# Gated DeltaNet layer: the 16x16 blocks of two visits solved in one set of vector operations

## The chip, the cores and the metric

The kernel runs on one core of a Trainium2 chip. The metric is the device time of one execution in microseconds (us). Five engines work side by side, each through its own queue in program order: PE (TensorE, matrix products; its weight loads are listed as PEld), DVE (VectorE), ACT (ScalarE), POOL (GpSimd) and SP (SyncE, which issues most transfers).

## What is computed

One layer over 2048 latent tokens and 256 context tokens of width 1024: a modulated LayerNorm, one wide projection, a branch A (gated DeltaNet with 8 heads of 128 in both directions), a branch B (gated short convolution), two output projections that are gated, merged and projected again, and a LayerNorm with the residual. The change lies in branch A:

```python
m = jnp.where(tri_strict, jnp.einsum('bhncd,bhnsd->bhncs', k_beta, k) * decay, 0.0)
eye = jnp.eye(CHUNK, dtype=jnp.float32)
t_inv = lax.linalg.triangular_solve(eye + m, jnp.broadcast_to(eye, m.shape), left_side=True, lower=True)
u = jnp.einsum('bhncs,bhnsv->bhncv', t_inv, v_beta)
w = jnp.einsum('bhncs,bhnsd->bhncd', t_inv, k_beta * jnp.exp(g_cum)[..., None])
...
def step(s, xs):
    qk_i, q_dec_i, k_dec_i, u_i, w_i, d_i = xs
    v_new = u_i - jnp.einsum('bhck,bhkv->bhcv', w_i, s)
    o = jnp.einsum('bhck,bhkv->bhcv', q_dec_i, s) + jnp.einsum('bhcs,bhsv->bhcv', qk_i, v_new)
    s = s * d_i[..., None, None] + jnp.einsum('bhck,bhcv->bhkv', k_dec_i, v_new)
    return s, o
```

The scan runs forward and backward over the same tokens. For each chunk and head a unit triangular matrix is inverted (lower in one direction, upper in the other).

## The kernel before, in words

Three stages follow each other. Up to about 1820 us the kernel computes the projections and writes their results to DRAM. Then comes the loop of branch A. After it `final` computes the last products.

The loop works on chunks of 128 tokens. A visit is one chunk in one direction, for all 8 heads; 18 chunks in two directions make 36 visits, forward (d = 0) and backward (d = 1) in turn. Each direction keeps its state `S`. A chunk that has been seen in the other direction takes its products of keys and queries from DRAM (`again`).

A visit needs, in this order: its keys and cumulative decays loaded (`visit_load`), the decay matrix `gcb` (`visit_decay`: eight operations of DVE at L140 between two exponentials of ACT, and a product `qd` on POOL at L138), the triangular matrix `N` (`gram`, products on PE, then L167 or L152 on DVE), the inverse of its 16x16 diagonal blocks (`inv_base`), the growth of the inverse from 16 to 32 (`inv_w16`, `inv_d16`), to 64 (`inv_w32`, `inv_d32`) and to 128 (`inv_w64`, `inv_d64`), the products of queries and keys (`gram` of `QK`), and then the steps with the state: `st_ks` (L299, its PSUM tiles emptied by DVE into `vh`, L301), `st_v` (L308), `st_o` (L319, L320) and `st_u` (L327, its PSUM tiles added to `S` by DVE, L332).

`inv_base` runs on DVE. The tile `n16` holds each block's negated strict triangle, 16 columns for 8 heads on 128 partitions. In 15 rounds a row of the growing inverse `R` is copied to all 16 rows of its block (L191, `stream_shuffle`), multiplied by a column of `n16` (L192) and added to `R` (L193). A round with w columns works on 8w elements of each partition, w from 1 to 15. Each of the three operations needs the one before it. At the end ACT spreads `R` to `r32` and DVE transposes it to `r32t` (L198).

The loop over i puts parts of several visits into one step: the state's part of visit i, the growth of the inverse of visit i + 1, `QK` of visit i + 2, and loads, decays, `N` and `inv_base` of visit i + 3. Between them `dense(n)` puts products of the output projections (L1230, L1232, L1234); `FILL` says how many of them a step takes, 24 in most, and a step before a repeated chunk takes 8 more. They run out where the next job's chunks are not yet normalised. All that is left runs after the loop.

PE's order is what the program writes (`manual_schedule`). The other engines' order is made by a planner at compile time, which takes the ready instruction that the program wrote first. PSUM tiles are in short supply: two each for `gram`, the inverse (`pinv`) and the state's products (`pst`), so PE waits where an earlier tile is not emptied yet.

## Time and profile before

| | us |
|---|---|
| median of 3 runs | 3288.05 |
| lowest and highest | 3284.26, 3294.42 |
| the profiled execution, its time | 3284.18 |
| its span, first to last instruction | 3282.5 |

The profile is of one execution. Times in its rows count from the start of the span. Busy time of an engine is the time in which at least one of its instructions ran; PE's matmuls overlap, so a mean duration is longer than the distance between two starts. PEclk is the clock that TensorE was granted, as a share of full speed.

### The profile page before, as it was taken

The page shows a single profiled execution, that of the slowest core. Times are in us where ns is not written, and L with a number is a line of the kernel's source. Part 1 is how long each engine was busy: PE and PEld are TensorE (multiplying, and loading weights), DVE is VectorE, ACT ScalarE, POOL GpSimd, SP SyncE. Part 2 cuts the span into 40 slices and gives each one's busy share as a digit, 9 for nine tenths or more (in the row PEclk, how much of TensorE's full clock was granted, in tenths as well). Part 3 has the DMA queues.
Part 4 walks back from the last instruction along what each step waited for, and adds up shares of the span by engine and source line. Part 5 has one row for each costly group of instructions (what it writes and reads, how often), then busy time and mean ns, then how long its engine had stood idle before and what let it go on. Part 6 is the DMA issues. An engine that isn't in the chain of part 4 may idle for free.

```text
span 3282.5 us, 60541 instructions
## 1 busy us (share of the span) xinstructions
PE 3011.9 (92%) x22089; PEld 2486.6 (76%) x22089; DVE 2294.7 (70%) x5815; ACT 1560.3 (48%) x3453; POOL 1622.7 (49%) x1156
## 2 busy tenths in 40 slices
PE   7899999999998899999999888988888888898987
PEld 4678778888886777888888677877777777786766
DVE  7656645555656564555632678999999898978699
ACT  4564633333456555333434355555555665654221
POOL 3444557765676454666665333344343233425464
PEclk9999999999999999999999889889989888999999
DMA  5433323224564432222333645465566667767742
GB/s 208 136 106 91 101 68 91 81 69 151 180 188 136 113 95 78 65 65 71 97 111 90 228 160 166 162 197 174 168 209 213 209 221 230 223 209 247 225 140 98
DMA packets 423047, 481.75 MB, mean 147 GB/s; under 512 B 25428, under 2 KB 324949, under 8 KB 421724
## 3 DMA queue, kind: packets, MB, share of 16 engines
q1 hardware_dynamic: 413646, 470.43, 45.8%
q10 hardware_dynamic: 9102, 7.45, 0.7%
q8 instruction: 173, 2.83, 0.4%
q14 instruction: 126, 1.03, 0.1%
HBM read 341.32 MB, written 136.47 MB: 146 GB/s over the span
## 4 chain that ended last, share of the span: by engine, by line
PE 50%; DVE 26%; issue 6%; ACT 5%; DMA 4%; POOL 4%; SPq 0%; DVEq 0%; ACTq 0%; POOLq 0%
PE pd L746 12%; PE pd L747 12%; PE pd L748 12%; DVE rb L192 3%; DVE gcb L140 3%; DVE R L193 2%; POOL al L352 2%; DVE rb L191 2%; DMA gcb<-gcd 2%; PE pf L1234 1%; PE pf L1230 1%; PE pf L1232 1%; DVE N L167 1%; PE pst L319 1%; ACT n L177 1%
## 5 line engine op out<-in xcount | busy, mean ns | idle before, releaser
L746 PE MATMUL pd<-bh,ah 128*128 128x512 f32 x2240 | 889.1, 397 | 9.9 <-ACT u L766 5.8
L748 PE MATMUL pd<-bh,al 128*128 128x512 f32 x2240 | 877.7, 392 | 0.0
L747 PE MATMUL pd<-bl,ah 128*128 128x512 f32 x2240 | 876.8, 391 | 0.0
L352 POOL TENSOR_TENSOR al<-s,ah 128x512 fp32r<-128x512 f32 x348 | 478.0, 1376 | 415.1 <-ACT ah L351 402.2
L352 POOL TENSOR_TENSOR al<-raw,ah 128x512 fp32r<-128x512 f32 x260 | 367.6, 1417 | 339.6 <-ACT ah L351 312.8
L746 PEld LDWEIGHTS pd<-bh,ah 128*128 128x128 f32 x2240 | 423.6, 189 | 98.1 <-issue 6.6
L748 PEld LDWEIGHTS pd<-bh,al 128*128 128x128 f32 x2240 | 423.2, 189 | 90.3 <-POOL al L352 0.4
L747 PEld LDWEIGHTS pd<-bl,ah 128*128 128x128 f32 x2240 | 423.6, 189 | 85.5
L351 ACT CAST ah<-s 128x512 fp32r<-128x512 f32 x352 | 215.4, 619 | 335.7 <-PE pd L747 311.2
L351 ACT CAST ah<-raw 128x512 fp32r<-128x512 f32 x264 | 162.4, 617 | 244.9 <-PE pd L747 206.5
L732 DVE TENSOR_TENSOR s<-s,raw 128x512 f32<-128x512 f32 x80 | 111.8, 1397 | 217.8 <-POOL s L732 217.8
L1234 PE MATMUL pf<-ah,wl 128*128 128x512 f32 x512 | 220.6, 431 | 5.6 <-DVE wl L352 3.5
L1230 PE MATMUL pf<-ah,wh 128*128 128x512 f32 x512 | 214.4, 419 | 10.5 <-DVE R L193 4.2
L1232 PE MATMUL pf<-al,wh 128*128 128x512 f32 x512 | 214.5, 419 | 6.1 <-DVE al L352 3.2
L352 POOL TENSOR_TENSOR wl<-wraw,wh 128x1024 fp32r<-128x1024 f32 x48 | 117.0, 2437 | 202.3 <-ACT wh L351 60.8
L192 DVE TENSOR_TENSOR rb<-rb,n 128x8 f32<-128x8 f32 (+6 forms) x540 | 199.9, 371 | 5.0
L140 DVE SCALAR_TENSOR_TENSOR gcb<-gcb,gc,mask 128x128 f32<-128x128 f32 x288 | 180.4, 631 | 6.8 <-ACT qd L137 5.6
L138 POOL TENSOR_TENSOR qd<-qd,qT 128x1024 f32<-128x1024 f32 x32 | 76.2, 2380 | 199.2 <-ACT qd L137 194.3
L193 DVE TENSOR_TENSOR R<-R,rb 128x8 f32<-128x8 f32 (+6 forms) x540 | 159.4, 296 | 5.6
L319 PE MATMUL pst<-S,qd 128*128 128x128 f32 x512 | 113.4, 307 | 36.5 <-ACT ot L1268 18.2
L1008 ACT ACTIVATE t<-t 128x512 f32<-128x512 f32 (+1 forms) x112 | 67.3, 601 | 138.1 <-DVE t L993 138.0
L771 DVE TENSOR_TENSOR u<-pd,u 128x512 f32<-128x512 f32 x80 | 55.0, 687 | 106.5 <-PE pd L748 97.5
(346 smaller groups left out, 6245.3 us busy)
## 6 DMA issues: line engine op xcount, KB each, us to landing
raw<-in_w_in SPq DMA_DIRECT2D x160, 512.0 KB, 3.9
kT<-kTd SPq DMA_DIRECT2D x36, 512.0 KB, 4.5
gcb<-gcd SPq DMA_DIRECT2D x36, 512.0 KB, 4.2
kt<-kd SPq DMA_DIRECT2D x36, 512.0 KB, 4.0
vh<-vd SPq DMA_DIRECT2D x36, 512.0 KB, 3.7
wraw<-in_w_b SPq DMA_DIRECT2D x32, 512.0 KB, 4.7
qT<-qTd SPq DMA_DIRECT2D x32, 512.0 KB, 3.9
wraw<-in_w_a SPq DMA_DIRECT2D x32, 512.0 KB, 4.5
```

Of the source, the lines that this page charges most:

```text
L140: nc.vector.scalar_tensor_tensor(out=gcb[:, h, :], in0=gcb[:, h, :], scalar=gcT[:, h:h + 1], in1=self.mask[d], op0=ALU.subtract, op1=ALU.min)
L192: nc.vector.tensor_tensor(out=rbv, in0=rbv, in1=bc(n16[:, :, i:i + 1], w), op=ALU.mult)
L193: nc.vector.tensor_tensor(out=R[:, :, c0:c1], in0=R[:, :, c0:c1], in1=rbv, op=ALU.add)
L319: nc.tensor.matmul(po[:, j, :], v["qd"][:, h, :], S[:, h, :], start=True, stop=False)
L351: self.nc.scalar.copy(out=hi, in_=src)
L352: (eng or self.nc.gpsimd).tensor_tensor(out=lo, in0=src, in1=hi.bitcast(F32), op=ALU.subtract)
L746: mm(ps, hi[:, k, :], bh, start=(first and k == 0), stop=False, skip_group_check=not first)
L747: mm(ps, hi[:, k, :], bl, start=False, stop=False, skip_group_check=not first)
L748: mm(ps, lo[:, k, :], bh, start=False, stop=(last and k == 3), skip_group_check=not first)
L1230: mm(ps, wh[:, k, :], ah, start=(k == 0), stop=False)
L1232: mm(ps, wh[:, k, :], al, start=False, stop=False)
L1234: mm(ps, wl[:, k, :], ah, start=False, stop=(k == KT - 1))
```

## The change

Two visits, one of each direction, are handed to `inv_base` together. The block of the backward visit is transposed first, so that both are lower triangular, and `n16` and `R` hold both, 16 columns for 16 heads. The rounds go by columns: row j of `n16` is copied to all rows of the block by the shuffle, multiplied by column j of `R` and added to the columns behind j. The shuffle of the next round is written between the multiply and the add of this one, and reads `n16`, not `R`. At the end the transposition that each visit had anyway is taken the other way round for the backward one.

For this `N` of a visit is made one step earlier (visit i + 4 in step i), as are loads, decays and `QK` (i + 3), and the tiles concerned get one more buffer. The loop begins at -4, with 24 dense products in that step. `inv_base` is called in every other step, for visits i + 3 and i + 4.

`inv_w16` reads `N` itself instead of the negated copy `n32`, and its result is negated. In `inv_w32` and `inv_d32` the products of different blocks follow each other head by head, where one block's eight heads came before the next block's; the transposed product is among them. The host call gives a smaller scratch for dynamic DMA.

```diff
-FILL = lambda i: {-3: 24, -2: 84, -1: 56}[i] if i < 0 else 24 if i < 16 else 24 if i < 25 else 27
+FILL = lambda i: {-4: 24, -3: 24, -2: 84, -1: 56}[i] if i < 0 else 24 if i < 16 else 24 if i < 25 else 27
...
-        v["kT"] = self.gk.tile([P, H, P], F32, name="kT", bufs=3)
+        v["kT"] = self.gk.tile([P, H, P], F32, name="kT", bufs=4)
...
-        v[name] = N = self.g2.tile([P, H, P], F32, name=name, bufs=2 if name == "N" else 3)
+        v[name] = N = self.g2.tile([P, H, P], F32, name=name, bufs=3 if name == "N" else 4)
...
-    def inv_base(self, v):
...
-        for i in (range(15, 0, -1) if d == 0 else range(0, 15)):
-            c0, c1 = (i, 16) if d == 0 else (0, i + 1)
-            w = c1 - c0
-            rbv = rb.rearrange("p h c -> p (h c)")[:, 0:H * w].rearrange("p (h c) -> p h c", c=w)
-            nc.vector.stream_shuffle(rbv, R[:, :, c0:c1], [i] * 16 + [16 + i] * 16)
-            nc.vector.tensor_tensor(out=rbv, in0=rbv, in1=bc(n16[:, :, i:i + 1], w), op=ALU.mult)
-            nc.vector.tensor_tensor(out=R[:, :, c0:c1], in0=R[:, :, c0:c1], in1=rbv, op=ALU.add)
...
+    def inv_base(self, va, vb):
+
+        nc, g2 = self.nc, self.g2
+        n16 = g2.tile([P, 2, H, 16], F32, name="n16", bufs=1)
+        for v in (va, vb):
+            n = g2.tile([P, H, 32], F32, name="n32", bufs=1)
+            for g in range(4):
+                s = slice(32 * g, 32 * g + 32)
+                nc.scalar.mul(out=n[s], in_=v["N"][s, :, s], mul=-1.0)
+            if v["d"]:
+                t = g2.tile([P, H, 32], F32, name="n32t", bufs=1)
+                nc.vector.transpose(self.fl(t), self.fl(n))
+                n = t
+            o = n16[:, v["d"]]
+            nc.scalar.mul(out=o, in_=n[:, :, 0:16], mul=self.m16[0])
+            nc.vector.scalar_tensor_tensor(out=o, in0=n[:, :, 16:32], scalar=self.m16[1], in1=o, op0=ALU.mult, op1=ALU.add)
+        n16 = n16.rearrange("p d h c -> p (d h) c")
+        rows = lambda t: t.unsqueeze(1).to_broadcast([P, 2 * H, 16])
+        nc.vector.tensor_tensor(out=n16, in0=n16, in1=rows(self.tri16), op=ALU.mult)
+
+        R = g2.tile([P, 2 * H, 16], F32, name="R16", bufs=1)
+        nc.gpsimd.tensor_copy(out=R, in_=rows(self.i16))
+
+        def row(j):
+            w = 15 - j
+            t = g2.tile([P, 2 * H * 15], F32, name="rb")[:, 0:2 * H * w].rearrange("p (h c) -> p h c", c=w)
+            nc.vector.stream_shuffle(t, n16[:, :, j + 1:16], [j] * 16 + [16 + j] * 16)
+            return t
+
+        nxt = row(0)
+        for j in range(15):
+            t, c = nxt, slice(j + 1, 16)
+            nc.vector.tensor_tensor(out=t, in0=t, in1=bc(R[:, :, j:j + 1], 15 - j), op=ALU.mult)
+            if j < 14:
+                nxt = row(j + 1)
+            nc.vector.tensor_tensor(out=R[:, :, c], in0=R[:, :, c], in1=t, op=ALU.add)
+        for v in (va, vb):
+            v["r32"] = r32 = g2.tile([P, H, 32], F32, name="r32", bufs=3)
+            v["r32t"] = r32t = g2.tile([P, H, 32], F32, name="r32t", bufs=3)
+            r, t = (r32t, r32) if v["d"] else (r32, r32t)
+            for hf in range(2):
+                nc.scalar.mul(out=r[:, :, 16 * hf:16 * hf + 16], in_=R[:, H * v["d"]:H * v["d"] + H], mul=self.m16[hf])
+            nc.vector.transpose(self.fl(t), self.fl(r))
...
-                nc.tensor.matmul(wp[s, h, :], v["n32"][s, h, :], v["r32t"][s, h, :], start=True, stop=True)
+                nc.tensor.matmul(wp[s, h, :], v["N"][s, h, s], v["r32t"][s, h, :], start=True, stop=True)
...
-        for p1, p2 in self.blocks(v["d"], 32):
-            for h in range(H):
+
+        for h in range(H):
+            for p1, p2 in self.blocks(v["d"], 32):
                 nc.tensor.matmul(wp[p2, h, :], v["N"][p1, h, p2], v["r32t"][p1, h, :], start=True, stop=True)
...
+        dt = self.pi.tile([P, H, 32], F32, name="pinv")
+        a, b = blks[lo], blks[1 - lo]
+        for h in range(H):
+            nc.tensor.matmul(dp[a[0], h, :], w32[a[1], h, :], r32[a[1], h, :], start=True, stop=True)
+            nc.tensor.matmul(dp[b[0], h, :], w32[b[1], h, :], r32[b[1], h, :], start=True, stop=True)
+            nc.tensor.matmul(dt[a[1], h, :], r32[a[1], h, :], w32[a[1], h, :], start=True, stop=True)
...
-            for i in range(-3, nv):
+            for i in range(-4, nv):
...
-                if v3:
-                    self.gram(v3, "N", v3["kT"])
-                    self.inv_base(v3)
-                if i > -3:
+                if v4:
+                    self.gram(v4, "N", v4["kT"])
+                    if v4["d"]:
+                        self.inv_base(v3, v4)
+                if i > -4:
                     dense(part[3])
```

## Rows read from the trace of the kernel before

**Rows 1.** The page's first part: busy us of each engine, share, instructions.

```profile
PE 3011.9 (92%) x22089; PEld 2486.6 (76%) x22089; DVE 2294.7 (70%) x5815; ACT 1560.3 (48%) x3453; POOL 1622.7 (49%) x1156
```

**Rows 2.** Stretches: us, busy PE, PEld, DVE, ACT, POOL (instructions), PEclk, DMA share, GB/s.

```profile
1820.00:1897.00 77.00, 61.88 (x552) 48.92 (x552) 57.60 (x224) 32.72 (x62) 28.30 (x17) 0.87 0.73 244
1897.00:2952.00 1055.00, 917.87 (x12562) 811.80 (x12548) 938.52 (x3642) 613.63 (x1451) 386.67 (x254) 0.92 0.60 195
```

**Rows 3.** Chain that ended last, 1900 to 2950 us: shares by line.

```profile
by line: DVE rb L192 9.4%; DVE gcb L140 8.5%; DVE R L193 7.1%; DVE rb L191 4.8%; DMA gcb<-gcd 4.0%; issue 3.5%; ACT n L177 3.3%; PE pst L319 3.3%; DVE N L167 2.9%; PE pst L320 2.6%; DVE QK L167 2.6%; PE pf L1234 2.4%; PE pst L327 2.1%; PE p
```

**Rows 4.** DVE's groups, 2000 to 2900 us: busy us, mean ns | idle before.

```profile
L192 DVE TENSOR_TENSOR rb<-rb,n 128x88 f32<-128x88 f32 (+14 forms) x440 | 159.1, 362 | 3.7
L140 DVE SCALAR_TENSOR_TENSOR gcb<-gcb,gc,mask 128x128 f32<-128x128 f32 x232 | 153.8, 664 | 5.6 <-ACT qd L137 5.6
L193 DVE TENSOR_TENSOR R<-R,rb 128x80 f32<-128x80 f32 (+14 forms) x441 | 125.7, 285 | 4.3
L191 DVE STREAM_SHUFFLE rb<-R 128x16 f32<-128x16 f32 (+14 forms) x440 | 97.3, 222 | 0.0
```

**Rows 5.** Stretch of 2000 to 2900 us, columns as in rows 2.

```profile
2000.00:2900.00 900.00, 781.08 (x10617) 690.95 (x10616) 815.42 (x3169) 522.35 (x1234) 333.65 (x220) 0.92 0.61 200
```

**Rows 6.** Timeline of DVE in one step: start us, us, instruction.

```profile
2297.14 0.34 DVE L167 SCALAR_TENSOR_TENSOR QK<-gram,cc,gcb 128x128 f32<-128x128 f32 x1
2297.40 0.17 DVE L192 TENSOR_TENSOR rb<-rb,n 128x16 f32<-128x16 f32 x1
2297.48 0.34 DVE L167 SCALAR_TENSOR_TENSOR QK<-gram,cc,gcb 128x128 f32<-128x128 f32 x1
...
2300.35 0.45 DVE L226 STREAM_TRANSPOSE r32t<-r 128x256 f32<-128x256 f32 x1
```

**Rows 7.** Timeline of DVE and POOL, 2306 to 2312 us.

```profile
2306.62 2.41 DVE L140 SCALAR_TENSOR_TENSOR gcb<-gcb,gc,mask 128x128 f32<-128x128 f32 x1
2308.96 2.43 DVE L192 TENSOR_TENSOR rb<-rb,n 128x96 f32<-128x96 f32 x1
...
2306.52 2.36 POOL L138 TENSOR_TENSOR qd<-qd,qT 128x1024 f32<-128x1024 f32 x1 [9.53 <-ACT qd L137]
2308.84 2.43 POOL L352 TENSOR_TENSOR wl<-wraw,wh 128x1024 fp32r<-128x1024 f32 x1
```

**Rows 8.** DVE's groups by shape, 1800 to 2960 us (15 shuffle shapes).

```profile
L198 DVE STREAM_TRANSPOSE r32t<-r 128x256 f32<-128x256 f32 x36 | 15.8, 440 | 13.7 <-ACT r L196 13.7
L182 DVE TENSOR_TENSOR n<-n,tri 128x128 f32<-128x128 f32 x36 | 14.0, 389 | 0.1
L191 DVE STREAM_SHUFFLE rb<-R 128x120 f32<-128x120 f32 x36 | 10.1, 281 | 0.0
L191 DVE STREAM_SHUFFLE rb<-R 128x8 f32<-128x8 f32 x36 | 5.8, 162 | 0.0
```

**Rows 9.** Groups of PE, 2000 to 2900 us, columns as in rows 4.

```profile
L319 PE MATMUL pst<-S,qd 128*128 128x128 f32 x464 | 103.8, 309 | 36.5 <-ACT ot L1268 18.2 <-DVE ot L1271 13.9 <-ACT v L311 4.3
L299 PE MATMUL pst<-S,kT 128*128 128x128 f32 x473 | 68.9, 295 | 30.1 <-DVE S L332 19.2 <-DVE ot L1271 10.8
L222 PE MATMUL pinv<-r,w 32*32 32x32 f32 x1856 | 23.1, 200 | 15.9 <-ACT w L213 15.9
```

**Rows 10.** Timeline of PE in one step, 2294 to 2311 us.

```profile
2294.44 0.75 PE L222 MATMUL pinv<-r,w 32*32 32x32 f32 x64 [1.19 <-ACT w L213]
...
2300.85 1.09 PE L246 MATMUL pinv<-r32t,N 32*32 32x32 f32 x32 [0.29 <-DVE r32t L226]
...
2305.50 1.00 PE L259 MATMUL pinv<-r,w32i 32*32 32x32 f32 x29
...
2306.43 0.57 PE L265 MATMUL pinv<-w32i,r 32*32 32x32 f32 x13
...
2310.58 0.39 PE L1234 MATMUL pf<-ah,wl 128*128 128x512 f32 x1
2310.81 0.39 PE L1230 MATMUL pf<-ah,wh 128*128 128x512 f32 x1
```

More of the change, by code (lines that the diff above doesn't have):

```diff
@@ L69, in consts @@
         nc.vector.reduce_sum(idx, pr, axis=AXX)
-        self.tri16 = []
-        for d, op in ((0, ALU.is_gt), (1, ALU.is_lt)):
-            t = pool.tile([P, 16], F32, name=f"tri{d}")
-            nc.vector.tensor_scalar(out=t, in0=io, scalar1=idx, scalar2=None, op0=op)
-            self.tri16.append(t)
+        self.tri16 = pool.tile([P, 16], F32, name="tri")
+        nc.vector.tensor_scalar(out=self.tri16, in0=io, scalar1=idx, scalar2=None, op0=ALU.is_gt)
         self.mask = []
@@ L256, in inv_d32 @@
         blks = self.blocks(d, 32)
-        for p1, p2 in blks:
-            for h in range(H):
-                nc.tensor.matmul(dp[p1, h, :], w32[p2, h, :], r32[p2, h, :], start=True, stop=True)
+        dt = self.pi.tile([P, H, 32], F32, name="pinv")
[4 more added lines that the diff above has]
+            nc.tensor.matmul(dt[a[1], h, :], r32[a[1], h, :], w32[a[1], h, :], start=True, stop=True)
         for p1, _ in blks:
             nc.scalar.mul(out=v["r64"][p1, :, c2], in_=dp[p1], mul=-1.0)
-        p1, p2 = blks[lo]
-        dt = self.pi.tile([P, H, 32], F32, name="pinv")
-        for h in range(H):
-            nc.tensor.matmul(dt[p2, h, :], r32[p2, h, :], w32[p2, h, :], start=True, stop=True)
+        p1, p2 = a
         nc.scalar.mul(out=v["r64t"][p2, :, c1], in_=dt[p2], mul=-1.0)
@@ L1305, in window @@
                     self.inv_w16(v1)
-                if v2 and v2["latent"]:
-                    self.gram(v2, "QK", v2["qT"])
-                if v2 and v2["again"]:
+                if v3 and v3["latent"]:
+                    self.gram(v3, "QK", v3["qT"])
+                if v3 and v3["again"]:
                     dense(8)
-                if v3:
-                    self.visit_load_q(v3)
+                if v4:
+                    self.visit_load_q(v4)
                 if v1:
                     self.inv_d16(v1)
-                if v3:
-                    self.visit_decay(v3)
+                if v4:
+                    self.visit_decay(v4)
                 if v0:
```

35 lines of the change are left out of this document (9 added, 26 removed).

## The prediction

> **What bounds the kernel now.** I read four views. The page first: PE is the busiest engine of the whole run [rows 1], which would say that a change on DVE buys nothing. A share of the whole run averages over stages, so the second view is the busy time by stretch [rows 2]. The stretch from the first product of `st_v` to the last visit's, 1897 to 2952 us, is the one that the change touches; it holds 35 steps from visit to visit of 1055 / 35 = 30.1 us each. In its middle, 2000 to 2900 us, DVE is busy 815.4 of 900 us and PE 781.1 [rows 5]: 27.3 and 26.2 us of a step. Neither is full, so the third view is the chain that ended last within the stretch [rows 3]: its four largest lines are DVE's, the three lines of the 16x16 solve (L191, L192, L193) and the decay line L140, 29.8% together. The fourth is what PE's groups wait for [rows 9]: the first products of a visit (L299) stood 30.1 us for DVE to empty PSUM tiles, those of `st_o` (L319) 36.5 us, 22.5 for ACT and 13.9 for DVE; L222 stood 15.9 us for ACT alone. So DVE sets the pace by its order of work, and PE is a close second, 1.1 us a step below it. That bound on the gain is the main thing to see here.
>
> **The solve on DVE.** Today each visit takes 15 rounds of shuffle, multiply, add, on 8w elements (8 heads, w = 1 to 15 columns). The shuffles show what such an operation costs undisturbed [rows 8]: 162 ns at 8 elements, 281 at 120, so (281 - 162) / 112 = 1.06 ns an element and 154 ns that do not depend on size. Fifteen take 15 x 154 + 1.06 x 960 = 3.33 us. Multiplies and adds cost the same where nothing holds them (0.17 us for 16 elements, [rows 6]). A visit: 3 x 3.33 = 10.0 us, two visits 20.0. Changed, two visits share 15 rounds on 16w elements: 3 x (15 x 154 + 1.06 x 1920) = 13.0 us. The elements are the same; 45 fixed costs are gone. That is 6.9 us a pair, 3.5 a visit, if each fixed cost is paid in full. It isn't always: where independent instructions alternate, the next starts 0.08 us before the last ends [rows 6], and then an operation removed gives back 0.154 - 0.08, 3.3 us a pair or 1.7 a visit. Between 1.7 and 3.5 I take 2.8, nearer to the upper end, because the new order carries its own independent neighbour (the next shuffle reads `n16`, not `R`, and stands between multiply and add), so more of the remaining operations overlap than today.
>
> **Preparation.** The second direction gains a transposition of 128x256, 0.44 us [rows 8]; the two multiplications by the triangle (0.39 us each) become one of twice the size, 0.39 + 128 x 1.06 ns = 0.53, so 0.25 less. Together +0.2 us a pair, 0.1 a visit. The ScalarE multiplications keep their number, with sign and mask moved; ACT is busy 522 of 900 us [rows 5] and hides them. The wait that is added: the first visit of a pair now waits for the second one's `N`. It was made a visit ahead for this, and its products are wanted only two visits later. Behind the waiting instruction on DVE stand `vh`, `QK` and `S`, which fill the time today too.
>
> **Stalls beside POOL.** A `gcb` operation that takes 0.34 us took 2.41, and the multiply after it 2.43 instead of about 0.26, exactly while POOL worked on `qd` and then `wl` [rows 7]. The means tell how often [rows 4]: L140 664 ns against 340, L192 362 and L193 285 against 222 for the shuffles of the same sizes. (324 x 232 + 140 x 440 + 63 x 441) ns = 165 us in 900, 5.5 us a step, half of POOL's 11.2 [rows 5]; 3.0 of it falls on the solve. If stalls go with the number of solve operations, half of that goes, 1.5; if each POOL instruction still meets one victim, nothing does. I take 0.7. The Trainium skill, "SBUF — State Buffer", section "SBUF: two separate sides", says that a VectorE operation with two SBUF inputs and a GpSimd operation that reads SBUF take a lock for the whole instruction and the later one is blocked. These rows agree on the length of a stall (2.4 us for 2.4). By that rule the stall belongs to the POOL instruction and not to the count of VectorE's, so it would put 0 for my 0.7, and the time would be 0.7 x 35 = 24 us higher; that is part of the second rival below.
>
> Sum for DVE: 27.3 - 2.8 + 0.1 - 0.7 = 23.9 us a step on average. It is not even: the pair's solve falls into every other step. Rounds (11 to 13 us), their stalls (some 2) and preparation (some 2) are 15 us, so the steps alternate between 23.9 + 7.5 = 31.4 and 16.4 us of DVE work.
>
> **Products in turn.** Today the 32-to-64 products run tile after tile: 32 matmuls in 1.09 us (L246), 48 in 1.50 from the first of L259 to the last of L265 [rows 10], 34 and 31 ns each. L222 takes four tiles in turn and needs 0.75 us for 64, 12 ns each. In turn over two tiles (L246) or over three products of which two share rows (L259, L265), the 80 matmuls cost between 80 x 12 ns = 0.95 us and today's 2.59. I take half of today's price, 17 ns: 1.36, a gain of 1.2 us a step. PE: 26.2 - 1.2 = 25.0. The Trainium skill, "TensorE: Matmul & The Clock Gate", section "Wait — 56ns, not 53.3ns?", has a floor of about 25 ns from start to start. That would leave only 0.6 us of the gain, but L222's 12 ns are below it, so the row decides.
>
> **Steps.** A light step is PE's: 25.0 plus the waits for ACT that stay, (15.9 + 18.2 + 4.3) / 29.9 steps = 1.3 [rows 9], 26.3 us. A heavy step has 31.4 us of DVE work, but its first part (both preparations, the vh of the next visit) can start in the light step's tail, where DVE has slack; what can't start early is what waits for the second `N`. I give 3 us to that, hence 28.4. Mean 27.4, 2.7 less than today: 35 x 2.7 = 95 us.
>
> **The ends.** The extra round ahead puts 24 more dense matmuls before the first visit, at 0.23 us from start to start [rows 10] 5.5 us. Against it the first two solves, which today keep DVE busy 57.6 of 77 us before the first visit [rows 2], become one; net +2, between -5 and +6. `gram` of QK is a visit further ahead too, its loads and stores with it: the SP queue issues the same transfers in the same order, only for another visit, and one more buffer each covers them. The 8 extra dense matmuls of repeated chunks start a visit earlier, the b jobs run out a visit earlier as well, and then dense work stops until chunks 6 to 9 are normalised. By the counts of `FILL`, the loop holds 1121 dense matmuls instead of 1129; 8 more fall into the end, +2 us. The end itself is untouched.
>
> Sum against the profiled execution (span 3282.5, its time 3284.2 us): 3284.2 - 95 + 2 + 2 = **3193 us**. The median of the three runs, 3288.05, is 3.9 us above that execution, so the forecast is 2.9% below the median, and 0.3%, 10 us, is about what a measurement of this kernel can tell from no change.
>
> **Rivals.**
> PE all through: if the heavy step's surplus fits into the light one's slack, every step is PE's, 25.5 to 26.3 us. For it: DVE's mean, 23.9, is below PE's 25.0, and the stretch's mean granted clock is 0.92 [rows 2], so a part of it ran at the lower level, 1.2 GHz. Against it: DVE runs in order, and the solve starts only behind the second `N`. 35 x 4.2 = 147 us less: 3141.
> Half of it: overlap hides more of the fixed cost than I think (1.7 instead of 2.8) and the stalls stay (0). Heavy steps are then 1.8 x 2 = 3.6 us longer, so the mean falls by 0.9 only: 3284 - 32 + 4 = 3256.
> Nothing of it: stretches of one visit's solve were spread over each step and filled waits; with the long operations DVE wins 3 us a pair, and PE loses as much waiting in heavy steps. For it: DVE and PE are only 1.1 us apart today. 3284, within 10 us.
> Slower: in a heavy step the solve has first call on DVE, as it was emitted first. Today an operation of another kind fits between any two solve operations, so eight `QK` and the two of `inv_d16` pass from 2297.1 to 2300.8, and L246, which needs them, waits 0.3 us [rows 6, 10]. In the new rounds the shuffle takes one of the three places, so only one stranger may pass per round of some 1.2 us; ten strangers take 12 us instead of 4. PE's few matmuls in between cover 2 us of that. L246 then stands about 6 us in every second step, and DVE runs dry later in the same step: 31.4 + 5 and 27 us, a mean of 31.5. 35 x 1.4 = +49: 3333. It decides where L246 waits more than some 5 us in a heavy step. Against it: the long first rounds only begin when `N` is through ACT, and much `QK` work can pass before.
>
> **How the numbers follow.** Forecast (3160 to 3230) 0.55, PE all through 0.17, half 0.13, nothing 0.06, slower 0.09. Faster by over 0.3% is the first three, 0.85; within 0.3% 0.06; slower 0.09. Leaving out the slower case, the empty one and the last of the PE case's gain, the range is 3125 to 3272. The likeliest case's own range is 3160 to 3230.
>
> **What would show it.** The solve's lines at about 13 us of DVE per pair, without stalls, under half as many instructions; shuffles of 240 elements near 0.41 us. DVE's share of the middle of the stretch below PE's. Steps alternating near 28 and 26 us. L246, L259 and L265 together under 1.6 us. L299's wait for DVE gone in light steps. It would be wrong if steps don't alternate, if L246's wait grows instead of L299's falling, or if PE waits for ACT take over what DVE gave back.

## The result, and the profile after

The changed kernel takes 3323.18 us (median, 3315.83 to 3327.75), the kernel before 3286.16 us beside it: ratio 1.0117, with a 95% interval of [1.0093, 1.0141]. It is 1.2% slower; the forecast of 3193 us and its range of 3125 to 3272 us are both missed.

The profiled execution after took 3315.83 us, with a span of 3314.1; it is the fastest of the four, so it shows 31.6 us of loss where the medians show 37. Its page, first part (busy us of each engine):

```profile
PE 2981.9 (90%) x22089; PEld 2447.3 (74%) x22089; DVE 2125.5 (64%) x4735; ACT 1565.9 (47%) x3453; POOL 1629.9 (49%) x1137
```

Both busy engines did less than in [rows 1], DVE by 169 us and PE by 30, and yet the span grew by 31.6 us. So the work did shrink, and waits took more than its place. The same stretches as in [rows 2, 5]: ahead of the first visit, the loop from visit to visit, and its middle.

```profile
1831.00:1916.00 85.00, 65.31 (x621) 51.73 (x620) 58.48 (x178) 39.43 (x75) 37.83 (x22) 0.88 0.75 248
1916.00:2978.00 1062.00, 875.18 (x12463) 770.88 (x12462) 780.47 (x2610) 610.96 (x1436) 374.55 (x232) 0.89 0.59 191
2000.00:2900.00 900.00, 734.80 (x10340) 646.82 (x10338) 664.55 (x2190) 509.71 (x1187) 319.96 (x196) 0.89 0.60 194
```

In the loop DVE is busy 780 us instead of 939 and PE 875 instead of 918, and the loop takes 7 us more. A part of PE's fall is work that left the loop: it holds 906 dense products instead of 938, because 24 went ahead of the first visit and 8 behind the last; at 0.23 us each that is some 7 us. Where the 31.6 us are: 9.6 in the projections ahead of the window (their last product starts at 1830.1 instead of 1820.5 us), 9.0 before the first visit, 6.8 in the loop, 6.3 after the last visit. The steps alternate, as forecast: in the loop 34.4 us for each step with a solve and 26.0 for each without, against 30.2 and 30.0 before. One such pair of steps (stretches as above):

```profile
2216.60:2254.10 37.50, 28.27 (x382) 25.63 (x376) 28.30 (x115) 18.35 (x37) 11.96 (x9) 0.86 0.44 146
2254.10:2280.40 26.30, 24.09 (x384) 21.77 (x376) 18.29 (x46) 14.67 (x31) 9.96 (x7) 1.00 0.61 196
```

In the light step PE works 24.1 of 26.3 us. In the heavy one neither engine is full: PE 28.3 and DVE 28.3 of 37.5 us. So it is first of all a matter of order, not of load. The groups of PE in the middle of the loop, with what they waited for (columns as in [rows 9]):

```profile
L332 PE MATMUL pst<-S,qd 128*128 128x128 f32 x448 | 98.9, 306 | 5.7 <-DVE ot L1284 3.0 <-ACT v L324 1.5 <-ACT ot L1281 1.2
L340 PE MATMUL pst<-v,kt 128*128 128x128 f32 x462 | 65.9, 289 | 21.1 <-DVE S L345 21.1
L312 PE MATMUL pst<-S,kT 128*128 128x128 f32 x456 | 60.6, 289 | 2.2 <-DVE ot L1284 2.2
L300 PE MATMUL pinv<-r,w 64*64 64x64 f32 x464 | 37.6, 239 | 26.7 <-ACT w L293 26.7
L259 PE MATMUL pinv<-r32t,N 32*32 32x32 f32 x928 | 22.7, 203 | 34.5 <-DVE r32t L238 34.5
L1412 PE MATMUL gram<-ident,ot 128*128 128x128 f32 x88 | 19.2, 362 | 26.7 <-ACT ot L1400 26.7
```

L332 and L312 are L319 and L299 of [rows 9]: their waits of 36.5 and 30.1 us fell to 5.7 and 2.2, which is what the forecast hoped for. In their place L259 (L246 of before), L300 and L340 wait, and L1412, which transposes normalised chunks. L259 and most of L300 stand in the first half of the loop, L340 and L1412 in the second. L259's wait is the one of [rows 10], 0.3 us then. Now PE in a heavy step:

```profile
2221.12 0.39 PE L332 MATMUL pst<-S,qd 128*128 128x128 f32 x2
2221.34 0.39 PE L333 MATMUL pst<-v,QK 128*128 128x128 f32 x2
2221.57 1.06 PE L340 MATMUL pst<-v,kt 128*128 128x128 f32 x8
2227.89 1.07 PE L259 MATMUL pinv<-r32t,N 32*32 32x32 f32 x32 [5.26 <-DVE r32t L238]
...
2229.47 0.64 PE L333 MATMUL pst<-v,QK 128*128 128x128 f32 x2
2229.90 0.63 PE L332 MATMUL pst<-S,qd 128*128 128x128 f32 x2
...
2242.24 1.14 PE L300 MATMUL pinv<-r,w 64*64 64x64 f32 x16 [3.63 <-ACT w L293]
```

and DVE in the same time:

```profile
2220.00 0.34 DVE L164 SCALAR_TENSOR_TENSOR QK<-gram,cc,gcb 128x128 f32<-128x128 f32 x1
2220.26 0.36 DVE L200 TENSOR_TENSOR rb<-rb,R 128x208 f32<-128x208 f32 x1
...
2220.55 0.37 DVE L194 STREAM_SHUFFLE rb<-n 128x192 f32<-128x192 f32 x1
2220.82 0.36 DVE L203 TENSOR_TENSOR R<-R,rb 128x208 f32<-128x208 f32 x1
2221.10 0.34 DVE L164 SCALAR_TENSOR_TENSOR QK<-gram,cc,gcb 128x128 f32<-128x128 f32 x1
...
2226.63 0.36 DVE L236 SCALAR_TENSOR_TENSOR r<-pinv,m16h,r 128x128 f32<-128x128 f32 x1
...
2227.38 0.45 DVE L238 STREAM_TRANSPOSE r32t<-r 128x256 f32<-128x256 f32 x1
```

Three operations of a round, then one stranger: eight `QK` go first, one per round of 0.8 to 1.1 us, then the two of `inv_d16` that L259 waits for. This is the mechanism of the "slower" rival. The stand costs a second time: the pairs of products behind it start 0.43 us apart (2229.47, 2229.90), where those ahead of it started 0.22 us apart (2221.12, 2221.34), so 0.21 and 0.11 us for each product. The granted clock of the heavy step is 0.86, of the light one 1.00; from 2226.3, within the stand, to 2233.1 us it is 0.50, which is 1.2 GHz. L259 stands 4.0 to 8.2 us in each of the eight heavy steps in which `QK` is made, 42.8 us together, and 0.3 us at most in any other step of the loop; the later visits load `QK` instead of making it, so no eight strangers queue ahead.

Late work runs on: `qd`'s exponential follows the late `st_o` on ACT, the decay's eight `gcb` follow it on DVE, their exponential on ACT ends at 2241.6, and only behind it in ACT's queue comes the copy that L300 waits for (3.63 us). This wait is not the order's alone: the eight `gcb` take 5.93 us here, because two of them take 1.96 and 2.48 us beside POOL's `wl` (2.37 us) and `qd` (2.46 us). Had these two taken 0.34 us like the other six, all would have been done an estimated 3.8 us earlier, which is as long as the wait; no run separates the two causes.

### The profile page after: what moved, and what is told of

The parts are those of the page before. It is cut to its first block, busy times and chain, and to the rows that moved or that the text cites. A ratio compares the mean times of both kernels' runs of the same rounds, so it can differ in the third digit from the quotient of the medians.

```text
span 3314.1 us, 59462 instructions
## 1 busy us (share of the span) xinstructions
PE 2981.9 (90%) x22089; PEld 2447.3 (74%) x22089; DVE 2125.5 (64%) x4735; ACT 1565.9 (47%) x3453; POOL 1629.9 (49%) x1137
## 4 chain that ended last, share of the span: by engine, by line
PE 52%; DVE 19%; issue 9%; DMA 6%; POOL 6%; ACT 4%; SPq 0%; DVEq 0%; POOLq 0%; ACTq 0%
PE pd L759 12%; PE pd L761 12%; PE pd L760 12%; POOL al L365 3%; DVE gcb L137 2%; DMA gcb<-gcd 2%; DVE R L203 2%; DVE rb L194 1%; DVE rb L200 1%; PE gram L155 1%; PE pf L1247 1%; POOL s L745 1%; DVE t L1004 1%; PE pf L1243 1%; PE pst L332 1%
## 5 line engine op out<-in xcount | busy, mean ns | idle before, releaser
L365 POOL TENSOR_TENSOR al<-raw,ah 128x512 fp32r<-128x512 f32 x260 | 376.5, 1450 | 329.0 <-ACT ah L364 289.3
L745 DVE TENSOR_TENSOR s<-s,raw 128x512 f32<-128x512 f32 x80 | 97.1, 1214 | 218.6 <-POOL s L745 199.5
L137 DVE SCALAR_TENSOR_TENSOR gcb<-gcb,gc,mask 128x128 f32<-128x128 f32 x288 | 188.0, 706 | 26.3 <-ACT qd L134 24.9
L1243 PEld LDWEIGHTS pf<-ah,wh 128*128 128x128 f32 x512 | 103.6, 202 | 41.3 <-issue 12.5
L1247 PEld LDWEIGHTS pf<-ah,wl 128*128 128x128 f32 x512 | 103.3, 202 | 34.5 <-DVE wl L365 10.8
L1245 PEld LDWEIGHTS pf<-al,wh 128*128 128x128 f32 x512 | 103.0, 201 | 32.2 <-DVE al L365 5.9
```

Of the source, the lines that this page charges most:

```text
L137: nc.vector.scalar_tensor_tensor(out=gcb[:, h, :], in0=gcb[:, h, :], scalar=gcT[:, h:h + 1], in1=self.mask[d], op0=ALU.subtract, op1=ALU.min)
L365: (eng or self.nc.gpsimd).tensor_tensor(out=lo, in0=src, in1=hi.bitcast(F32), op=ALU.subtract)
L745: eng.tensor_tensor(out=o, in0=a, in1=b, op=op)
L1243: mm(ps, wh[:, k, :], ah, start=(k == 0), stop=False)
L1245: mm(ps, wh[:, k, :], al, start=False, stop=False)
L1247: mm(ps, wl[:, k, :], ah, start=False, stop=(k == KT - 1))
```

## The experiments

Each is the changed kernel, or the kernel before, with the edit shown. The planner orders each engine's queue by priority: operations under `high_priority(600)` come earlier in it, under a negative number later. All ratios are against the kernel before, run beside it. Stages of the profiled execution, in us: start of the last product of the projections, from there to the first visit (its first product of `st_v`), mean step of the first 18 and of the last 17, and the end behind the last visit's `st_v`.

| kernel | ratio [95%] | proj. | to first visit | steps 1-18 | steps 19-35 | end |
|---|---|---|---|---|---|---|
| before | 1 | 1821 | 77 | 30.9 | 29.3 | 330 |
| after | 1.0117 [1.0093, 1.0141] | 1830 | 86 | 31.1 | 29.5 | 336 |
| e1_turn_only | 0.9944 [0.9922, 0.9965] | 1815 | 78 | 30.2 | 29.1 | 329 |
| e2_ahead_alone | 0.9997 [0.9981, 1.0012] | 1818 | 92 | 30.3 | 28.7 | 337 |
| e3_d16_first | 0.9995 [0.9981, 1.0010] | 1827 | 89 | 28.1 | 30.6 | 336 |
| e4_solve_last | 1.0206 [1.0180, 1.0233] | 1825 | 89 | 31.8 | 30.5 | 337 |
| e5_pad | 1.0096 [1.0075, 1.0117] | 1816 | 86 | 31.2 | 29.6 | 339 |
| e6_pad_fill0 | 1.0083 [1.0065, 1.0100] | 1817 | 89 | 31.3 | 29.4 | 336 |
| e7_state_first | 1.0018 [1.0007, 1.0029] | 1817 | 88 | 29.9 | 29.7 | 336 |
| e8_gate_first | 1.0051 [1.0033, 1.0069] | 1814 | 88 | 30.7 | 29.8 | 338 |
| e12_d16_pad | 0.9951 [0.9934, 0.9968] | 1816 | 89 | 28.3 | 30.7 | 337 |
| e9_both_first | 0.9855 [0.9832, 0.9877] | 1817 | 83 | 27.0 | 29.4 | 339 |
| e13_turn_order | 0.9925 [0.9907, 0.9943] | 1820 | 78 | 29.7 | 29.2 | 330 |
| e15_ahead_order | 0.9936 [0.9913, 0.9958] | 1820 | 90 | 29.3 | 28.9 | 336 |
| e10_half_each | 0.9898 [0.9876, 0.9920] | 1817 | 84 | 27.7 | 29.6 | 337 |
| e11_half_later | 0.9823 [0.9805, 0.9842] | 1820 | 88 | 27.4 | 29.0 | 339 |
| e14_half_gone | 0.9766 [0.9734, 0.9798] | 1817 | 82 | 27.5 | 27.6 | 339 |
| e16_norm_first | 0.9844 [0.9824, 0.9864] | 1819 | 86 | 26.9 | 29.0 | 337 |

**The parts of the change.** e1 is the kernel before with the products in turn:

```diff
-        for p1, p2 in self.blocks(v["d"], 32):
-            for h in range(H):
+        for h in range(H):
+            for p1, p2 in self.blocks(v["d"], 32):
```

> The kernel before with one part of the change alone: the products of inv_w32 and inv_d32 in turn. In the changed kernel these take about 0.7 us (inv_w32) and 0.7 to 0.9 us (inv_d32) where they took 1.09 and 1.50. If this part is harmless and PE is not the bound of a step (theory), the time stays within 25 us below the kernel before, 3260 to 3290. If taking the products in turn is itself what made the changed kernel slower (rival), it is above 3300.

e2 is the changed kernel with each visit solved by itself again, row by row, with the `inv_base` and the two masks of before (cut here), still made a visit ahead:

```diff
-                    if v4["d"]:
-                        self.inv_base(v3, v4)
+                    self.inv_base(v4)
```

> The changed kernel with each visit solved by itself, as before the change, at the end of the step that makes its N; everything else stays as changed (N one visit ahead, the first step at -4, products in turn, N as weights of inv_w16). Theory (the solve of two visits in one step stands before the operations that PE waits for): steps do not alternate, the waits of inv_w32 for r32t fall from 43 us to below 10, and the time is 3255 to 3295. Rival (the deeper look-ahead costs: order of ACT and POOL, buffers, the extra first step): still 3310 to 3330, with the first visit as late.

The products in turn alone give 0.56%. The look-ahead on top (e2 against e1) costs 0.5%: 3 us in the projections, 14 us to the first visit and 8 at the end, 3 less in the loop. e2's steps no longer alternate: 29.2 us for the even and 29.8 for the odd ones; L259's wait (L247 in e2) is 13.7 us in the loop, above the 10 that were expected. So the loss of the change lies in the pair and the look-ahead, and the products in turn are not the cause.

**The order of DVE's queue.** e3 and e4:

```diff
+        with self.tc.high_priority(600):       # e3; inv_d16's two operations
             nc.vector.scalar_tensor_tensor(out=r32[:, :, cs], ...)
             nc.vector.transpose(self.fl(r32t), self.fl(r32))
...
+        with self.tc.high_priority(-600):      # e4; the rounds
             for j in range(15):
```

> The changed kernel, but the two operations of inv_d16 on DVE (multiply-add and transposition of r32) are put before the rounds of the solve; QK keeps its place. Theory: inv_w32 waits below 12 us in sum instead of 43, the heavy step falls from 34.4 us on average to 31 to 32.5, and the time to 3265 to 3295. If the heavy step is bound by the sum of DVE's work or by ACT (rival), the wait moves to another line and the time stays 3310 to 3330.

> The changed kernel, but the rounds of the solve get a lower priority, so that QK, inv_d16, the decays and the updates of S go before them whenever they are ready. Theory: no wait of PE for r32 of inv_d16, and PE gains 4 us in every second step, 3240 to 3290; the price is that r32t of the solve comes later, so the waits of inv_w16 rise from 3 us to 20 to 60. Rival (the heavy step is bound by the sum of DVE's work): 3310 to 3330 in whatever order.

e3 takes 40 us off: the wait before L259 (here L260) is gone and L300's (here L301) is down from 26.7 to 6.0, in the same stretch of 2000 to 2900 us:

```profile
L313 PE MATMUL pst<-S,kT 128*128 128x128 f32 x480 | 70.9, 304 | 28.2 <-DVE S L346 23.7 <-DVE ot L1285 4.5
...
L301 PE MATMUL pinv<-r,w 64*64 64x64 f32 x480 | 37.9, 235 | 6.0 <-ACT w L294 6.0
...
L260 PE MATMUL pinv<-r32t,N 32*32 32x32 f32 x928 | 20.1, 192 | 0.0
```

L313 is L312 of after: its wait is back at 28.2 us, near the 30.1 of before. So its fall to 2.2 was no gain; PE had stood earlier in the step instead. And the 40 us are a difference: the first 18 steps are 54 us shorter than in after, the last 17 are 17 us longer, which the gate product's order takes back below (e9 against e12, 21 us there).

With the solve last of all (e4) I expected a gain and got the slowest kernel: now the next step's first inverse products wait for the solve's own result.

```profile
L223 PE MATMUL pinv<-r32t,N 32*32 32x32 f32 x1728 | 24.5, 215 | 92.1 <-DVE r32t L211 75.5 <-DVE kd L129 11.0 <-DVE t L125 5.7
```

So the solve may be neither first nor last in these kernels. e7 moves the state's and the v update ahead as well (pad below included):

```diff
+            with self.tc.high_priority(600):   # st_ks: vh; st_u: S
                 for h in range(4 * g, 4 * g + 4):
```

> The padded kernel in which three groups of VectorE operations go ahead of the pair's solve in VectorE's queue: the two of inv_d16, the four of each half of the state update, and the four of each half of the v update. Order theory: what is left of the loss stands in waits of TensorE for these (30 us before the state products, 21 us before the update products and 23 us before the v products in the run that moved inv_d16 alone); half of that goes, the loop from first to last state product is 985 to 1015 us (1061.7 in the changed kernel, 1024.8 with inv_d16 alone moved), the time 3235 to 3260 us, ratio 0.986 to 0.993. Rival (VectorE's sum in the heavy step is the bound, so that whatever goes first delays the rest): the waits come back at the decay and the 64-row merge, the loop is 1020 to 1040 us and the ratio 0.995 to 1.000.

The rival is nearer: ratio 1.0018, above its bound. PE no longer waits for what was moved, but the solve's result is late, as in e4 (loop, 1904 to 2948 us), and the transpositions of normalised chunks (L1416) stand 62.2 us:

```profile
L223 PE MATMUL pinv<-r32t,N 32*32 32x32 f32 x2176 | 29.5, 210 | 78.6 <-DVE r32t L211 69.1 <-DVE kd L130 9.5
```

**The stage that the change does not touch.** The projections ended 9.6 us later. The constant mask `tri1` of the kernel before is gone, 16 columns of 4 B, so that everything laid out behind it should stand 64 B lower. e5 puts an unused tile in its place, e6 also leaves out the 24 dense matmuls of the first lead step:

```diff
+        pool.tile([P, 16], F32, name="tripad")          # e5, e6
-FILL = lambda i: {-4: 24, -3: 24, ...
+FILL = lambda i: {-4: 0, -3: 24, ...                     # e6
```

> The changed kernel plus one unused tile of 16 columns (64 B per partition) behind the one constant mask that it has left, so that all tiles that are laid out behind it stand where the kernel before has them. No operation is added. Address theory: in the projection stage, which the change does not touch, the matmuls of the changed kernel start 229.06 ns apart, against 227.14 ns before; with the pad they are back at 227.1 ns, the last projection matmul ends at 1816 to 1821 us (1830.1 in the changed kernel), and the time falls by 10 to 13 us, to a ratio of 1.007 to 1.009 against the kernel before. Rival (the spacing differs for another reason, such as the chip or the instruction order): spacing stays at 229 ns and the ratio at 1.012.

> The padded kernel without the 24 dense matmuls that the change adds in the first of its four lead steps; these matmuls are then issued later, since the list of dense work is the same. If the longer prologue (85.2 us against 76.2 from the last projection to the first state product) is made of these 24 matmuls, it falls by about 5 us (24 times 0.23 us) and the time by 3 to 6 us against the padded kernel, or not at all where the work comes back in the tail. If it is made of waits for VectorE (one of 9.7 us stands there in the trace of the changed kernel), the matmuls only filled that wait, and prologue and time stay within 2 us.

The projections' products between 600 and 1750 us, in the kernel before, after and in e5 (one of three alike groups each):

```profile
L746 PE MATMUL pd<-bh,ah 128*128 128x512 f32 x1562 | 617.2, 395 | 5.8 <-ACT u L766 5.8
```

```profile
L759 PE MATMUL pd<-bh,ah 128*128 128x512 f32 x1549 | 617.1, 398 | 5.7 <-ACT u L779 5.7
```

```profile
L760 PE MATMUL pd<-bh,ah 128*128 128x512 f32 x1562 | 617.5, 395 | 5.8 <-ACT u L780 5.8
```

In the same 1150 us 1562 products pass in the kernels with the old addresses and 1549 in the changed one; from start to start 227.1 and 229.1 ns. With the pad the projections end 13.7 us earlier. All three kernels without the tile or the mask (after, e3, e4) have the wider spacing, and their last product starts at 1825 to 1830 us; the fifteen others have the narrower one, and 1814 to 1821 us. So the missing tile is the cause, and since it adds no operation, the addresses are; why 64 B matter to these products was not found out. Of e5's 13.7 us the loop and the end take back 8, and the ratio falls by 0.2%, which is not clear of noise, as the two intervals overlap. e6 shows that the 24 dense matmuls are not what makes the way to the first visit longer: without them PE waits that time (89 us against 86). What does make it longer stays open.

**Together.** e8 moves the product with the gate, which frees the bank of a dense matmul, ahead of the solve (`evac_b`, with the pad); e9 has pad, gate product and `inv_d16` first; e12 is e9 without the gate product.

```diff
+            with tc.high_priority(600):
                 nc.vector.scalar_tensor_tensor(out=gt, in0=gt, scalar=1.0, in1=ps, ...)
```

> The padded kernel in which the one VectorE operation that takes a dense result of the b jobs out of its bank (the product with the gate, evac_b) goes ahead of the pair's solve in VectorE's queue. In the padded kernel's prologue TensorE stands 9.7 us before a dense matmul for this operation, because the first pair's solve is in front of it (the kernel before stood 4.3 us there). If that wait is what makes the prologue longer (85.4 us from the last projection to the first state product, against 76.2 before), it goes to under 3 us, the prologue falls by 6 to 9 us and the time by about as much, to a ratio of 1.0065 to 1.008. Rival (the solve itself must end before the first state product, and the wait only lies where the chain has slack): the stand moves to a later matmul, prologue and time stay within 2 us of the padded kernel's.

> The three edits together: the pad, the gate product ahead of the solve, and inv_d16's two operations ahead of the solve. It is the best that the pair with its look-ahead gives with the order mended. If the terms add up (40 us for inv_d16's order, 6 to 7 us for the pad, 0 to 9 us for the gate product), the time is 3260 to 3275 us, ratio 0.994 to 0.998, the steps about 31.4 and 27 us. Rival: the terms overlap, and it stays at the 0.9995 of inv_d16's order alone.

> The changed kernel with the pad and inv_d16's two operations first, without the gate product's order: what is left out of both_first is that order alone. Together the three edits gave 89 us where alone they gave 40 (inv_d16), 7 (pad) and 13 (gate product beside the pad). If the gate product's order is what gives more once inv_d16's wait is gone (in the loop it stands in front of each dense matmul of the b jobs whose bank it frees), this kernel is at 3265 to 3272 us, ratio 0.995 to 0.9975, its loop near 1025 us. If the pad does it (addresses reach the loop as well), the loop is near 990 us and the ratio 0.986 to 0.989.

e8 does not shorten the way to the first visit, as its rival said: the wait of 9.7 us becomes 3.2 before the dense matmul and 4.5 before the first inverse products. The gain lies in the loop, and at 1.0051 it is larger than the 1.0065 to 1.008 expected. e9 takes 3234.26 us, faster than both kernels, and gains more than the sum of its parts: against e12 the loop is 46 us shorter, of which TensorE's idle time gives 22.6 (157.0 to 134.4) and its busy time 23.6 (875.0 to 851.4) for the same products, the mean granted clock of the loop being 0.93 instead of 0.90. Fewer stands came with a higher clock. Heavy and light step of e9, at the same place as those of after:

```profile
2219.50:2247.70 28.20, 25.35 (x378) 21.64 (x377) 28.20 (x107) 16.67 (x34) 11.51 (x8) 1.00 0.58 191
2247.70:2272.70 25.00, 24.40 (x385) 21.72 (x377) 17.92 (x53) 16.31 (x35) 10.65 (x7) 1.00 0.60 206
```

and PE in that heavy step (start us, us, instruction):

```profile
2225.28 1.06 PE L342 MATMUL pst<-v,kt 128*128 128x128 f32 x8
2226.26 0.69 PE L261 MATMUL pinv<-r32t,N 32*32 32x32 f32 x32
```

28.2 and 25.0 us (28.4 and 25.5 in the mean of the first 18 steps), where the prediction had 28.4 and 26.3. L261 (L259 of after) follows L342 with no wait.

**What the pair is worth.** e13 is e1 with e9's two orders, e15 is e2 with them.

> The kernel before with the 32-to-64 products in turn and the same two orders as both_first (inv_d16's two operations and the gate product first), without the pair, the columns and the look-ahead. It says what the pair itself is worth. Theory that the order is worth something only because the pair's solve is one block of 13 to 20 us in VectorE's queue: here the rounds of a single visit are shorter blocks, the orders give 0 to 10 us against the 0.9944 of the products in turn alone, ratio 0.991 to 0.9945, and the pair is worth 18 to 30 us to both_first. Rival (the orders help any kernel, the pair is worth nothing): ratio 0.983 to 0.988, as both_first.

> The kernel with the look-ahead and the products in turn in which each visit is solved by itself, row by row (ahead_alone), with the two orders of both_first. Against both_first only the pair solved by columns is missing; against turn_order the look-ahead is added. If the gain of both_first over turn_order (0.9855 against 0.9925) is the pair's, this kernel stays at 0.990 to 1.000. If it is the look-ahead's, which lets the solve stand back at no price, it reaches 0.984 to 0.988.

0.9925 and 0.9936 against e9's 0.9855: with the order mended the pair is worth 0.7 to 0.8%, some 25 us; the look-ahead alone is worth nothing. Without the mended order, and with the addresses of before in both (e5 against e2), the pair costs 1.0%. The two orders matter most to the pair: they give it 2.4% (e5 to e9), the single solves with the look-ahead 0.6% (e2 to e15), and those without it 0.2% (e1 to e13), which is within the noise.

**The unequal steps.** e10 and e11 were to move half of the rounds into the light step, e14 leaves them out; in all three the inverse lacks the odd rounds. The edit, shortened:

```diff
-        for j in range(15):
+        rounds(R, range(0, 15, 2))                # e10, e11, e14
+        self.rest = lambda: rounds(R2, range(1, 15, 2))   # e10, e11; called at the end of the next step, at the start of the one after
```

> As the run with both_first, but each pair's 15 rounds are split over its two steps: the even rounds as before, on the real operand, and the odd ones in the next step on a tile that nobody reads. So the inverse leaves out the odd rounds, while the operations, their shapes and their number over two steps are the same (one more copy on GpSimd). About 7 us of VectorE's work go from the heavy step into the light one. Theory that the unequal steps eat the gain (the heavy step is set by VectorE, the light one by TensorE, and what TensorE has to spare in the heavy one can't be carried over): the two steps come out within 2 us of each other, at 27 to 28.5 us, the loop is 960 to 1000 us, the time 3205 to 3240 us. Rival (the steps are set by the chain of the state and of the inverse through all engines, which is the same in both, not by VectorE's sum): the mean step stays at 29 us, the loop at 1020 to 1035 us, the time within 8 us of both_first's.

> As half_each, whose odd rounds were meant for the light step and, by its trace, ran 16 to 20 us into the heavy one; here they are issued one more step later, so that they fall into the light step. The odd rounds are again made on a tile that nobody reads, and the inverse leaves them out. Number and shapes of the operations are those of half_each. Theory of the unequal steps (the heavy one set by VectorE, the light one by TensorE): heavy falls from 30.4 by up to 7 us to TensorE's 25.4 and its other waits, light stays at 26 to 27, the loop at 930 to 970 us, time 3170 to 3215 us. Rival (chain of the state through all engines): heavy 29 to 31, light 26 to 28, the loop at 980 to 1010 us, time 3225 to 3255 us.

> both_first with the odd rounds of each pair's solve left out altogether (the inverse leaves them out), so that some 7 us of VectorE's work and of the solve's own chain are gone from each heavy step, and nothing comes in their place. It is the upper bound of what half_each and half_later were to show, since in those the planner put the odd rounds back into the heavy step. Theory that the heavy step is VectorE's: it falls from 30.4 us by 3 to 5 us, the loop to 910 to 940 us, time 3150 to 3185 us. Rival (the heavy step is TensorE's 25 us and its waits in the chain of the state): it falls by less than 1.5 us, the loop stays above 960 us, the time above 3205 us.

e10 and e11 did not do what they were meant to. In e10's heavy step that begins at 2287.9 us and lasts 30.4, the last real round and the first of the others:

```profile
2296.12 0.18 DVE L206 TENSOR_TENSOR R<-R,rb 128x16 f32<-128x16 f32 x1
...
2306.18 0.37 DVE L206 TENSOR_TENSOR R16b<-R16b,rb 128x224 f32<-128x224 f32 x1
```

Nothing waits for these rounds, so they came where DVE had room, 18 to 20 us into the same step in the first half of the loop, in e11 too. They say nothing on unequal steps, which stays open. e14's loop is 964.7 us, near its rival's bound and far from the 910 to 940 of the theory. Its first and second half:

```profile
1898.90:2394.60 495.70, 445.42 (x6585) 394.94 (x6577) 359.68 (x1103) 301.61 (x618) 215.60 (x147) 0.94 0.62 199
2394.60:2863.70 469.10, 404.45 (x5887) 351.57 (x5883) 339.99 (x1030) 304.36 (x818) 153.63 (x85) 0.92 0.69 222
```

and the same halves of before, after and e9:

```profile
1897.40:2453.80 556.40, 480.76 (x6594) 429.34 (x6584) 497.34 (x1902) 305.33 (x623) 219.91 (x160) 0.91 0.53 175
2453.80:2952.30 498.50, 436.71 (x5936) 382.09 (x5923) 441.36 (x1740) 308.30 (x828) 166.76 (x95) 0.92 0.68 218
```

```profile
1916.00:2475.40 559.40, 461.47 (x6578) 414.64 (x6576) 401.46 (x1357) 305.22 (x618) 216.94 (x147) 0.89 0.53 174
2475.40:2977.70 502.30, 413.41 (x5891) 355.94 (x5883) 378.71 (x1254) 305.75 (x818) 157.61 (x85) 0.90 0.65 209
```

```profile
1899.80:2385.10 485.30, 439.17 (x6584) 383.70 (x6576) 407.84 (x1356) 299.94 (x618) 215.91 (x147) 0.96 0.61 203
2385.10:2885.60 500.50, 412.20 (x5892) 356.22 (x5883) 382.14 (x1254) 306.08 (x818) 159.32 (x85) 0.89 0.64 208
```

e14 takes 48 us more of DVE's work out of the first 18 steps than e9, and they get no shorter (495.7 against 485.3 us); the last 17 are 31 us shorter. So in the first half DVE's load is not what is left, although DVE is busy all 28.2 us of the heavy step above. In the second half the heavy steps fall from 32.4 us (e9) to 28.8, so the pair's rounds still stand before something there; before what, no run shows.

**The second half of the loop.** e9 gains 71 us over before in the first 18 steps and nothing in the last 17, though these hold only 458 dense products where before had 498. e16 is e9 with the normalisation's twelve short DVE operations first.

> both_first with the twelve short VectorE operations of a chunk's normalisation (rms and reciprocal root, 128x8 each) ahead of the solve as well. In both_first the last 17 steps of the loop gained nothing (500.5 us against 498.5 before), and TensorE stood 32.3 us there before the transpositions of normalised chunks, three times for 8 to 12 us, against 8.1 before. Theory that the pair's rounds stand ahead of these twelve operations: the 32 us fall to under 12, the last 17 steps to 475 to 485 us, the time to 3210 to 3225 us, ratio 0.978 to 0.983. Rival (the wait is the chain's own length, twelve operations in a row behind each other and behind GpSimd's work): it stays above 25 us and the time within 6 us of both_first's.

The wait before the transpositions of normalised chunks is gone (PE's groups, 2385 to 2886 us):

```profile
L1416 PE MATMUL gram<-ident,ot 128*128 128x128 f32 x112 | 17.2, 304 | 0.0
```

but the last 17 steps fall by 8 us only (492.9): TensorE stands before the v products, the update products and the 64-row merge instead. The cause of this wait was the order, as the theory said; its price was not 32 us, and at 3228.82 us the time missed the 3210 to 3225 expected. e16 is within e9's interval, and lies 1.6% below the kernel before. Why the second half gains no more is open.

## Why the prediction was wrong

**The step that failed** is the heavy step of 28.4 us in **Steps**. It was got from DVE's sum of 31.4 us, less 3 for what can start early, as if PE's needs were served in time. In after a heavy step takes 34.4 us in the mean, 36.3 in the first half of the loop, with DVE busy 28.3 us of the one shown. In the first half the solve's place in the queue is why: e3, which moves two operations per visit and removes none, gives 40 us back. The prediction had this as its "slower" rival. The trace has its stand, 4.0 to 8.2 us where about 6 was said, but in eight steps and not in every second one. It had a chance of 0.09, on the argument that much `QK` work would pass before the rounds begin; in the trace the first `QK` passes 2.1 us after the first shuffle. [Rows 6] had shown one stranger between any two solve operations; the step from there to one stranger per round was made and then set aside. That the rival's 3333 us lies near the result is luck: it put 49 us into the loop, which lost 7, while 25 us were lost elsewhere, and its own steps of 36.4 and 27 us have a mean of 31.7 and not 31.5, which makes 3340.

**What held.** The solve: 13.0 us a pair was forecast; the lines L194, L200 and L203 take (61.4 + 66.0 + 67.6) / 14 = 13.9 in the middle of the loop. DVE's groups of after, 2000 to 2900 us, columns as in [rows 4]:

```profile
L137 DVE SCALAR_TENSOR_TENSOR gcb<-gcb,gc,mask 128x128 f32<-128x128 f32 x224 | 159.6, 766 | 24.1 <-ACT qd L134 24.0
L203 DVE TENSOR_TENSOR R<-R,rb 128x240 f32<-128x240 f32 (+14 forms) x210 | 67.6, 322 | 0.2
L200 DVE TENSOR_TENSOR rb<-rb,R 128x240 f32<-128x240 f32 (+14 forms) x210 | 66.0, 314 | 0.1
L194 DVE STREAM_SHUFFLE rb<-n 128x240 f32<-128x240 f32 (+14 forms) x210 | 61.4, 299 | 0.0
```

DVE fell from 26.8 us a step of the loop to 22.3, more than the 3.4 forecast. The light step: 26.3 forecast, 26.0 measured. The products in turn: L259 took 0.69 us in a light step, and the 48 of L273 to L275 0.70. PE's timeline of after:

```profile
2259.47 0.69 PE L259 MATMUL pinv<-r32t,N 32*32 32x32 f32 x32
...
2262.07 0.21 PE L273 MATMUL pinv<-r,w32i 32*32 32x32 f32 x1
...
2262.58 0.19 PE L275 MATMUL pinv<-w32i,r 32*32 32x32 f32 x1
```

1.39 us where 1.36 was forecast and 2.59 stood in [rows 10]. In the heavy step shown above, at 1.2 GHz, L259 took 1.07 us. But e1 shows what 1.2 us a step of PE are worth while DVE's order sets the pace: 18 us of the 42, by its median.

**Stalls beside POOL.** -0.7 us a step was forecast. By the groups above, and 289 ns for an undisturbed solve operation (the forecast's 13.0 us / 45), the stalls come to an estimated 426 ns x 224 + (25 + 33) ns x 210 = 108 us in 900, 3.6 a step, against 165 and 5.5: the solve's share went nearly all, the `gcb` operations' rose from 324 to 426 ns each. The Trainium skill, "SBUF — State Buffer", section "SBUF: two separate sides", says that of two such operations the later one is blocked for the whole of the other. The prediction read it as one stall for each POOL instruction, and so no change. POOL's busy time hardly moved (334 and 320 us) and a third of the stalled time went. So the trace agrees with the rule on who may be stalled (the two `gcb` operations beside `wl` and `qd` above), but the rule does not tell how often.

**Mis-sized or unseen.** Of the 123 us between the forecast and the profiled execution, 102 lie in the loop, about half in each half of it. The ends: +2 and +2 us were forecast, +9.0 and +6.3 came. e2 has them too and e1 does not, so they belong to the look-ahead; the 24 dense matmuls, which the prediction priced at 5.5, do not make the way to the first visit longer (e6). The prediction counted them there and not as work that leaves the loop; its 1129 and 1121 dense matmuls in the loop are 938 and 906 in the traces. The projections: nothing was forecast, +9.6 came, through addresses (e5). The second half: 2.7 us a step, worked out from the means of 2000 to 2900 us and rows at 2294 to 2312 us, were carried to all 35; in the last 17 not even e9 gains. That is 17 x 2.7 = 46 of the 95 us. L259 does not stand there; e14 says that the pair's rounds still cost there, and the rest of the cause stays open. In the first 18 steps e9 reaches (28.4 + 25.5) / 2 = 27.0 us a step, where the prediction had 27.4: its sum comes out for that half once the order is mended.

## What to carry to other kernels

When a change joins many short operations into one block, work out what stands behind the block in its engine's queue and which other engine waits for that; give those few operations a place ahead, but not so many that the block itself comes late. A saving of engine time is worth only what the waits let through: here the same joined block cost 1.0% in one order and gave 0.7 to 0.8% in another. A wait that vanishes is no gain by itself: see whether PE only stood earlier. Look at a rate per step in each part of the loop before multiplying it by the number of steps.

## What the runs showed that was not expected

Where a 64-byte tile was left out, 128x512 products in a stage that was not changed went from 227.1 to 229.1 ns apart, 0.9%; an unused tile in its place undid it.

32x32 products in turn over several tiles started closer than the forecast's 17 ns: 48 of them within 0.51 us from the first start to the last, 11 ns apart, where 31 ns were needed tile after tile.

A stand of some 5 us was paid twice: the granted clock of the heavy step was 0.86 instead of 1.00, and the 128x128 products behind the stand started 0.21 us apart instead of 0.11.
